# The rarely taken branch of the first MoE at two places: behind the last expert, and behind the fourteenth

## The chip, the cores and the metric

The kernel runs on one core of a Trainium2 chip. The metric is device time in microseconds of one launch. Engines are named as in the profile: PE multiplies matrices (PEld loads its weights, PEq is its sequencer), DVE, ACT and POOL work on vectors, and SP issues most DMA transfers.

## What is computed

Two blocks of two layers each on 256 tokens of width 1024. The change lies in the first block, of which each layer is a token mixer with memory attention, a layer norm, a mixture of experts and a layer norm:

```
def first_block(x, ...):
    for i in range(DEPTH):                       # two layers
        ...                                      # mixer and attention
        x = layer_norm(ALPHA * x + o, ln1_g[i], ln1_b[i])
        f = grouped_moe(x, router_w, router_b, w_gate[i], w_up[i], w_down[i])
        x = layer_norm(ALPHA * x + f, ln2_g[i], ln2_b[i])

def grouped_moe(x, router_w, router_b, w_gate, w_up, w_down):
    ...                                          # combine: two experts of 16 per token
    for e in range(N_EXPERTS):
        h = jax.nn.silu(xt @ w_gate[e]) * (xt @ w_up[e])
        out = out + combine[:, e:e + 1] * (h @ w_down[e])
```

A token goes to two of 16 experts (hidden width 512), so an expert gets some 32 tokens of the 256 on average.

## The kernel before

`moe1` (L923) works off one layer's 16 experts in the loop over `e` at L1025. Tokens of four experts at a time are gathered into at most CAP1 = 64 slots per expert by matmuls with a 0/1 matrix (`gather`). Then come, one iteration apart: `gate_up(e)` (matmuls into tile `gu`, 64 slots against chunks of weights), `hidden(e)` (transposes `tr`), `down(e - 1)` (matmuls `yps`, then tiles `sy` scaled by ACT and DVE) and `scatter(e - 1)`, eight matmuls that add the expert's rows into the four PSUM tiles `ya`. `gate_up` also makes the slot numbers of its expert (`slps`). The tiles `sy` stand in two rooms of the pool `p_c`, tags "lng" and "lnb" (L1013).

The weights come as chunks of 1 MB, six per expert, which SP issues in the order of use (L76) as soon as one of 18 buffers is free (12 called `raw`, 6 called `whl`). Behind the last expert's chunks SP issues the next stage's dense weights and the layer norm's parameters `lngb` (L362).

An expert that more than 64 tokens have chosen is finished by `rest1` (L1065): `most` leaves the largest count in `bigi`, four engines (`BRANCH`: PE, DVE, ACT and SP) read it into a register (L1068), and `tc.If(rv > CAP1)` (L1069) guards a body that runs all 16 experts densely over the tokens left over. With these inputs the body is never taken. Each of the four engines still goes through the `If`: it reads the register, compares, and jumps past the body to a short piece of code that waits until the engine itself (for SP: every transfer that was issued) has finished, adds to the semaphores what the body would have added, and goes on. The scheduler, which otherwise orders instructions by when they can run, moves none across an `If`.

`rest1` is called once per layer, behind the loop (L1041). What follows is `ln_banks` (L505): 24 matmuls on constants that only keep PE running (`warm`, L533), and then for each half t of the tokens: statistics of `ya` on DVE (`bnst`, L521), a chain of small DVE operations that ends in the normalized `pre` (L515), its transposes on PE (`lnT`, L535), their copies on ACT (`xf`, L536) and the first matmuls of the next stage (`begin`). In layer 1 the next stage's first instructions also stand there: on DVE `lp` (L1154), on ACT the DMA issues `gup` (L1132), `strict` and four of `bias` (L1267).

Of the kernel before, what the change touches and what calls it, by code (L numbers as in the profile page):

```python
# [21 lines left out]
T = 256  # L22
ALPHA = 4.0 ** 0.25
E1, F1, CAP1 = 16, 512, 64
# [12 lines left out]
BRANCH = [ET.PE, ET.DVE, ET.Activation, ET.SP]  # L37
# [13 lines left out]
class Stream:  # L51
# [4 lines left out]
    def __init__(self, k, chunks, ahead=1, limit=None, room=None):  # L56
        self.k, self.chunks, self.ahead = k, chunks, ahead
        self.p_raw, self.p_hl, self.small = room or k.p_raw, k.p_hl, room is not None
        self.loaded, self.done, self.pos, self.pool, self.deep = 0, 0, 0, [], 0
        self.raw, self.ready, self.room = [], [], {}  # L60
        self.limit = len(chunks) if limit is None else limit
# [72 lines left out]
class Banks:  # L134
# [5 lines left out]
    def tile(self, shape, dt, name, tag=None):  # L140
        if self.pool is not None and tag not in self.tags:
            return self.pool.tile(shape, dt, name=name, tag=tag)
        self.n += 1
        return self.k.p_ps.tile(shape, dt, name=name, tag=f"b{self.banks[self.n % len(self.banks)]}")


class Begin:
# [81 lines left out]
class Kern:  # L229
# [693 lines left out]
    def moe1(self, layer, stream, x, xt, fill, began, begin):  # L923


        nc, tc = self.nc, self.tc
        pre = self.p_x.tile([128, 2, D], F32, name="pre", tag="x")
        part = lambda e: e == 0 and fill is None
        with ExitStack() as st:
            pool = st.enter_context(tc.tile_pool(name=f"moe{layer}", bufs=1))  # L930
            with ExitStack() as st2:
# [4 lines left out]
                cb, pm, cnt = self.route1(pool, pp, lg)  # L936
# [10 lines left out]
            bigi = self.most(pool, cnt)  # L947
# [3 lines left out]
            bank = lambda t, c: ya[t][c]  # L951
            with ExitStack() as st2:
# [61 lines left out]
                def scatter(e):  # L1014
                    for t in range(2):
                        for c in range(2):
                            if e == 0:
                                self.mm(ya[t][c], self.ident, pre[:, t, half(c, 512)], True, False)
                        for i in range(2):
                            for c in range(2):  # L1020
                                r = half(c, 64)
                                self.mm(ya[t][c], slots[e][0][r, half(t)], ys[e][i][r, :], False, e == E1 - 1 and i == 1)
                    del slots[e], ys[e]

                for e in range(E1 + 1):  # L1025
# [12 lines left out]
                        gb = self.load_ln(2 * layer + 1)  # L1038
                    if e > 0:
                        scatter(e - 1)  # L1040
            self.rest1(layer, bank, x, cb, pm, bigi, part)  # L1041
            xt = self.ln_banks(pre, bank, gb, Banks(self, (0, 1)), begin)
        return pre, xt

# [17 lines left out]
        self.nc.vector.tensor_tensor(w, w, cb, op=OP.mult)  # L1062
        return w

    def rest1(self, layer, bank, x, cb, pm, bigi, part):  # L1065

        nc, tc = self.nc, self.tc
        rv = nc.values_load(bigi[0:1, 0:1], engines=BRANCH, min_val=0, max_val=T)  # L1068
        with tc.If(rv > CAP1):  # L1069
            with ExitStack() as st:  # L1070
                p1 = st.enter_context(tc.tile_pool(name=f"rest{layer}", bufs=1))
                pg, py = Banks(self, (0, 1)), Banks(self, (2, 3))
                room = st.enter_context(tc.tile_pool(name=f"rr{layer}", bufs=2))
                wt = self.left(p1, pm, cb, CAP1, E1)
                xt = self.turned(x, pg, "rg", True)
                for e in range(E1):
                    fs = (1,) if part(e) else (0, 1)
                    w = Stream(self, self.chunks1(layer, e, [j for f in fs for j in (2 * f, 2 * f + 1, 4 + f)]), ahead=0, room=room)
                    self.dense1(w, xt, wt, e, fs, bank, p1, pg, py)
# [572 lines left out]
    def moe2(self, stream, x, xt, began, ln, out):  # L1652
# [5 lines left out]
        with ExitStack() as st:  # L1658
# [191 lines left out]
            def total(t, c, tile):  # L1850
                bank[t][c] = tile()
                self.mm(bank[t][c], self.ident, pre[:, t, half(c, 512)], True, False)
# [21 lines left out]
            for (t, c), tile in zip(halves, tiles):  # L1874
                at(i + 3, total, t, c, tile)
# [349 lines left out]
```

## Time and profile before

| | us |
|---|---|
| three runs | 1952.04, 1956.91, 1957.87 (median 1956.91) |
| profiled execution | 1956.97, of which the span is 1955.2 |
| first MoE, the expert loop up to the last `ya`, layer 0 | about 144 to 386.73 |
| the same, layer 1 | about 530 to 757.36 |
| PE busy over the whole span | 1822.1 (93%) |

The profile is one execution. The span is the time from the first instruction to the last, and the launch has 1.8 us around it. Its times of day ("at 386.73") count from the span's start. [...] DMA is the mean busy share of 16 DMA engines.

### The profile page before, as it was taken

To read this page: it belongs to the slowest core of one execution; us is meant where nothing else is said; L and a number is where in the kernel's file an instruction comes from. 1 tells how busy PE (TensorE), PEld (TensorE's weight loads), DVE (VectorE), ACT (ScalarE), POOL (GpSimd) and SP (SyncE) were. 2 spreads that over 40 slices of the span, in tenths; PEclk is the share of its full clock that TensorE was granted. 3 is DMA by queue.
4 is the path that set the end of the run, shared out by engine and by line. 5 is a ranking of instruction groups with operands and counts; after the bars stand their busy time and mean duration, and the time that the engine had idled before them with its cause. 6 is when DMAs were issued, how large, how long until landed. Compare 5 with 4: busy or idle time off the path is not lost. (4 is left out here: it accounts for less than half of the span.)

```text
span 1955.2 us, 36295 instructions
## 1 busy us (share of the span) xinstructions
PE 1822.1 (93%) x15228; PEld 1424.6 (73%) x15228; DVE 892.0 (46%) x1631; ACT 735.9 (38%) x1205; POOL 297.8 (15%) x129
## 2 busy tenths in 40 slices
PE   9999999899999998998999988899998889999896
PEld 8885555488655555897999867787777778987753
DVE  5661121267411113467101476655556568866412
ACT  5531111054211111652444364344445456655311
POOL 0310000002000000523888323200000000000000
PEclk9999999999999999999999999899999999999898
DMA  9659999855598894744553240489999999899995
GB/s 381 249 193 409 409 419 419 326 198 191 192 414 347 340 419 168 288 169 159 181 187 130 88 177 23 172 323 391 388 416 418 418 419 415 343 391 419 419 415 231
DMA packets 86031, 589.29 MB, mean 301 GB/s; under 512 B 9782, under 2 KB 11510, under 8 KB 16340
## 3 DMA queue, kind: packets, MB, share of 16 engines
q1 hardware_dynamic: 83042, 580.67, 74.6%
q10 hardware_dynamic: 2802, 6.06, 0.9%
q8 instruction: 126, 2.06, 0.4%
q14 instruction: 61, 0.50, 0.1%
HBM read 585.45 MB, written 1.24 MB: 300 GB/s over the span
## 5 line engine op out<-in xcount | busy, mean ns | idle before, releaser
L103 ACT ACTIVATE whl<-raw 128x1024 fp32r<-128x1024 f32 x426 | 433.1, 1054 | 220.4 <-issue 98.4
L105 DVE TENSOR_TENSOR whl<-raw,whl 128x1024 fp32r<-128x1024 f32 x315 | 375.2, 1228 | 128.1 <-ACT whl L103 125.8
L105 POOL TENSOR_TENSOR whl<-raw,whl 128x1024 fp32r<-128x1024 f32 x111 | 274.3, 2489 | 898.5 <-ACT whl L103 845.2
L287 PE MATMUL sgu<-whl,xe 128*128 128x256 f32 x2064 | 261.2, 287 | 27.2 <-DVE sh L1705 21.5
L287 PEld LDWEIGHTS sgu<-whl,xe 128*128 128x128 f32 x2064 | 252.7, 193 | 36.4 <-DVE sh L1705 26.5
L287 PE MATMUL gu<-raw,xe 128*64 128x256 f32 x1408 | 172.4, 382 | 0.0
L287 PEld LDWEIGHTS gu<-raw,xe 128*64 128x64 f32 x1408 | 102.0, 137 | 53.7 <-issue 5.3
L287 PE MATMUL fgu<-xh,whl 128*128 128x256 f32 x640 | 116.7, 283 | 0.0
L287 PE MATMUL zps<-xh,whl 128*128 128x256 f32 x576 | 111.5, 291 | 2.6 <-ACT xh L276 1.8
L990 ACT ACTIVATE h<-gu 128x256 f32<-128x256 f32 x31 | 11.9, 383 | 253.6 <-PE gu L287 253.6
L1948 POOL TENSOR_TENSOR pre<-pre,lngb 128x512 f32<-128x512 f32 x2 | 2.5, 1259 | 672.5 <-ACT pre L1947 672.5
L287 PEld LDWEIGHTS fgu<-xh,whl 128*128 128x128 f32 x640 | 100.3, 192 | 0.4
L991 DVE TENSOR_TENSOR h<-h,gu 128x256 f32<-128x256 f32 x31 | 13.1, 422 | 184.8 <-ACT h L990 184.8
L287 PEld LDWEIGHTS zps<-xh,whl 128*128 128x128 f32 x576 | 92.8, 195 | 3.9 <-ACT xh L276 2.0
L287 PE MATMUL fgu<-xl,whl 128*128 128x256 f32 x320 | 90.4, 283 | 0.0
L287 PE MATMUL yps<-raw,hT 128*64 128x512 f32 x352 | 89.5, 595 | 0.0
L287 PE MATMUL zps<-xl,whl 128*128 128x256 f32 x288 | 82.7, 287 | 0.8 <-DVE xl L277 0.8
L287 PE MATMUL sy<-whl,shh 128*128 128x512 f32 x264 | 82.7, 394 | 0.0
L1688 ACT ACTIVATE sh<-sgu 128x256 f32<-128x256 f32 x43 | 16.5, 383 | 159.1 <-PE sgu L287 159.1
L317 DVE SCALAR_TENSOR_TENSOR sy<-yps,gs,sy 128x512 fp32r<-128x512 f32 x32 | 24.0, 751 | 113.7 <-ACT sy L316 113.7
L287 PE MATMUL gu<-whl,xe 128*64 128x256 f32 x608 | 75.5, 383 | 0.0
L1380 DVE TENSOR_TENSOR fh<-fh,fgu 128x512 f32<-128x512 f32 x10 | 6.9, 689 | 139.7 <-PE fgu L287 139.7
(490 smaller groups left out, 3180.5 us busy)
## 6 DMA issues: line engine op xcount, KB each, us to landing
raw<-in_w_moe_dram SPq DMA_DIRECT2D x399, 1024.0 KB, 11.9
whl<-in_w_moe_dram SPq DMA_DIRECT2D x57, 1024.0 KB, 11.0
raw<-in_w_dense_dram SPq DMA_DIRECT2D x53, 1024.0 KB, 7.0
raw<-in_w_ffn_dram SPq DMA_DIRECT2D x33, 1024.0 KB, 6.0
lngb<-in_lnp_dram ACTq DMA_DIRECT2D x8, 512.0 KB, 4.5
lngb<-in_lnp_dram SPq DMA_DIRECT2D x8, 512.0 KB, 5.0
xraw<-in_xT_dram SPq DMA_DIRECT2D x4, 256.0 KB
raw<-in_w_dense_dram SPq DMA_DIRECT2D x2, 512.0 KB, 4.7
```

What stands on the lines that cost most here:

```text
L103: nc.scalar.activation(hi, r, AF.Copy)
L105: on.tensor_tensor(lo, r, hi, op=OP.subtract)
L287: self.nc.tensor.matmul(out, lhsT, rhs, start=start, stop=stop, skip_group_check=True)
L317: self.nc.vector.scalar_tensor_tensor(yl, ps, gate, yh, op0=OP.mult, op1=OP.subtract)
L990: nc.scalar.activation(h, ps[:, 0, :], AF.Silu)
L991: nc.vector.tensor_tensor(h, h, ps[:, 1, :], op=OP.mult)
L1380: nc.vector.tensor_tensor(h, h, g[1], op=OP.mult)
L1688: nc.scalar.activation(h, ps[:, 0, :], AF.Silu)
L1948: nc.gpsimd.tensor_tensor(v, v, gb[0][:, half(c, 512)], op=OP.mult)
```

## The change

The register is read at the end of the iteration e = 11 (`E1 - 5`), and the `If` stands at the end of the iteration e = 13 (`E1 - 3`), so behind `scatter(12)` and `hidden(13)` and ahead of `gate_up(14)`: twelve chunks, those of the experts 14 and 15, are issued behind it. The body's weights, which stood in two buffers of a pool of their own, take the two rooms "lng" and "lnb" in turn. The body itself is the same. Lines of the changed kernel stand 11 to 14 lower.

```diff
+class InTurn:
+    def __init__(self, pool, tags):
+        self.pool, self.tags, self.n = pool, tags, 0
+
+    def tile(self, shape, dt, name, tag=None):
+        self.n += 1
+        return self.pool.tile(shape, dt, name=name, tag=self.tags[self.n % len(self.tags)])
...
                     if e > 0:
                         scatter(e - 1)
-            self.rest1(layer, bank, x, cb, pm, bigi, part)
+                    if e == E1 - 5:
+                        rv = nc.values_load(bigi[0:1, 0:1], engines=BRANCH, min_val=0, max_val=T)
+                    if e == E1 - 3:
+                        self.rest1(layer, bank, x, cb, pm, rv, part)
             xt = self.ln_banks(pre, bank, gb, Banks(self, (0, 1)), begin)
...
-    def rest1(self, layer, bank, x, cb, pm, bigi, part):
+    def rest1(self, layer, bank, x, cb, pm, rv, part):
         nc, tc = self.nc, self.tc
-        rv = nc.values_load(bigi[0:1, 0:1], engines=BRANCH, min_val=0, max_val=T)
         with tc.If(rv > CAP1):
...
-                room = st.enter_context(tc.tile_pool(name=f"rr{layer}", bufs=2))
+                room = InTurn(self.p_c, ("lng", "lnb"))
```

Three places show what moves. The first is SP in layer 0, from the last two of the MoE's chunks on. Before, the branch stands behind all chunks of the MoE, one dense chunk and the two transfers of `lngb` (`_49` in a wait only numbers the program's semaphores):

```order
L76 DMA raw<-in_w_moe_dram 128x2048 [waits DMAHW4_49,PE_49]
L76 DMA raw<-in_w_moe_dram 128x2048 [waits DMAHW5_49,PE_49]
L76 DMA raw<-in_w_dense_dram 128x2048 [waits DMAHW6_49,PE_49]
L362 DMA lngb<-in_lnp_dram 128x1024 [waits DMAHW7_49,PE_49]
L362 DMA lngb<-in_lnp_dram 128x1024 [waits DMAHW0_49]
L1068 TENSOR_LOAD bigi [waits DVE_49,PE_49,Activation_49]
L1069 COMPARE_AND_BRANCH
```

Now the last chunk of expert 13 stands ahead of the branch:

```order
L76 DMA raw<-in_w_moe_dram 128x2048 [waits DMAHW6_49,PE_49]
L76 DMA raw<-in_w_moe_dram 128x2048 [waits DMAHW7_49,PE_49]
L76 DMA raw<-in_w_moe_dram 128x2048 [waits DMAHW0_49,PE_49]
L76 DMA raw<-in_w_moe_dram 128x2048 [waits DMAHW1_49,PE_49]
L1082 COMPARE_AND_BRANCH
```

and what the engine finds behind the body are the chunks of the experts 14 and 15, of which these are the first seven:

```order
L76 DMA whl<-in_w_moe_dram 128x2048 [waits DMAHW2_49,PE_49]
L76 DMA whl<-in_w_moe_dram 128x2048 [waits DMAHW3_49,PE_49]
L76 DMA whl<-in_w_moe_dram 128x2048 [waits DMAHW4_49,PE_49]
L76 DMA whl<-in_w_moe_dram 128x2048 [waits DMAHW5_49,PE_49]
L76 DMA whl<-in_w_moe_dram 128x2048 [waits DMAHW6_49,PE_49]
L76 DMA whl<-in_w_moe_dram 128x2048 [waits DMAHW7_49,PE_49]
L76 DMA raw<-in_w_moe_dram 128x2048 [waits DMAHW0_49,PE_49]
```

So twelve chunks have moved from the front of the branch to its back. The second place is PE in layer 0 where the branch stands now, between the last four `ya` of `scatter(12)` and, behind the body, the slot numbers and the first `gu` of expert 14:

```order
L298 MATMUL ya_1593<-sy,sT 128x512 [waits DVE_49]
L298 MATMUL ya_1594<-sy,sT 128x512
L298 MATMUL ya_1595<-sy,sT 128x512
L298 MATMUL ya_1596<-sy,sT 128x512
L1053 TENSOR_LOAD bigi [waits DVE_49,PE_49,Activation_49]
L1082 COMPARE_AND_BRANCH
```

and behind the body (the second row of the branch's end is where the four engines add up their counts):

```order
L1082 UNCONDITIONAL_BRANCH
L1082 UNCONDITIONAL_BRANCH [waits PE_49]
L855 MATMUL slps<-consts,pm 128x128 [waits PE_49,Activation_49]
L855 MATMUL slps<-consts,pm 128x128
L855 MATMUL slps<-consts,cb 128x128 x2
L298 MATMUL gu<-raw,xe 64x256 [waits DMAHW0_49,PE_49]
```

Before, those rows of `ya` and `slps` followed each other with nothing between them. The third place is PE at the end of the loop in layer 0. Before, the last `ya` are followed by the branch, and all 24 `warm` stand behind the body:

```order
L287 MATMUL ya_1593<-sy,sT 128x512 [waits DVE_49]
L287 MATMUL ya_1594<-sy,sT 128x512
L287 MATMUL ya_1595<-sy,sT 128x512
L287 MATMUL ya_1596<-sy,sT 128x512
L1068 TENSOR_LOAD bigi [waits DVE_49,PE_49,Activation_49]
L1069 COMPARE_AND_BRANCH
```

and behind the body:

```order
L1069 UNCONDITIONAL_BRANCH
L1069 UNCONDITIONAL_BRANCH [waits PE_49]
L287 LDWEIGHTS bfconst
L287 MATMUL warm<-bfconst 128x256 [waits Activation_49]
L287 LDWEIGHTS bfconst
```

Now no branch stands there, and nine of the 24 `warm` have moved ahead of the last eight `ya`, two of them between the halves of `yps` and seven behind it:

```order
L298 MATMUL yps<-raw,hT 64x512 [waits DMAHW5_49]
L298 MATMUL yps<-raw,hT 64x512 x3
L298 LDWEIGHTS bfconst
L298 MATMUL warm<-bfconst 128x256
L298 LDWEIGHTS bfconst
L298 MATMUL warm<-bfconst 128x256
```

The other 15 follow the last `ya` at once:

```order
L298 MATMUL ya_1593<-sy,sT 128x512 [waits DVE_49]
L298 MATMUL ya_1594<-sy,sT 128x512
L298 MATMUL ya_1595<-sy,sT 128x512
L298 MATMUL ya_1596<-sy,sT 128x512
L298 LDWEIGHTS bfconst
L298 MATMUL warm<-bfconst 128x256
```

What moved there is the branch, which is gone from between `ya` and `warm`. Layer 1 moves in the same way on both engines.

## Rows read from the trace of the kernel before

**Rows 1.** Waits of PE, both layers' loops: line, waited for, us in total, times, longest

```profile
PE ya L287 <- ACT sy L316: 6.3, 9, 0.8
...
PE ya L287 <- ACT sy L316: 5.5, 8, 0.8
```

**Rows 2.** Waits of SP's sequencer, layer 0's loop to its end

```profile
SPq L76 <- PE gu L287: 145.2, 29, 11.9
...
SPq L1069 <- SPq L1069: 11.6, 1, 11.6
```

**Rows 3.** Windows in both loops: each engine's busy time, PEclk, DMA share, GB/s

```profile
339.70:353.10 13.40, 12.56 (x92) 6.44 (x92) 2.09 (x5) 1.34 (x3) 0.00 (x0) 1.00 1.01 418
...
710.30:723.70 13.40, 12.56 (x92) 6.45 (x92) 2.09 (x5) 1.34 (x3) 0.00 (x0) 1.00 1.01 419
```

**Rows 4.** The branch's instructions, layer 0: duration ns min/median/max, first and last start

```profile
L1069 SPq EVENT_SEMAPHORE  x8: 17/17/17, 360.4 to 360.9; - x8
...
L1069 PEldq COMPARE_BRANCH  x1: 6233/6233/6233, 386.7 to 386.7; - x1
```

**Rows 5.** The same view, layer 1

```profile
L1069 PEldq COMPARE_BRANCH  x1: 3549/3549/3549, 757.2 to 757.2; - x1
```

**Rows 6.** Windows at both ends of the loop, columns as in rows 3

```profile
386.73:389.73 3.00, 0.00 (x1) 0.00 (x0) 2.86 (x11) 0.00 (x0) 0.00 (x0) 0.89 1.02 423
389.73:393.11 3.38, 0.00 (x0) 0.03 (x1) 3.31 (x11) 0.00 (x0) 0.00 (x0) 0.50 0.53 206
393.11:396.96 3.85, 3.85 (x24) 2.87 (x25) 3.64 (x16) 0.00 (x0) 0.00 (x0) 0.64 0.02 4
...
757.36:760.87 3.51, 0.00 (x0) 0.03 (x1) 1.09 (x2) 0.00 (x0) 0.00 (x0) 1.00 0.04 9
760.87:765.15 4.28, 4.28 (x24) 3.20 (x25) 4.07 (x18) 0.00 (x0) 0.00 (x0) 0.60 0.32 88
...
767.90:771.30 3.40, 3.36 (x11) 2.89 (x12) 3.29 (x12) 0.84 (x3) 0.00 (x0) 0.50 0.23 62
```

**Rows 7.** Timeline of PE at layer 0's end: start, length, what, [idle before]

```profile
393.11 4.12 PE L287 MATMUL warm<-bfconst 128*128 128x256 bf16 x24 [6.38 <-PEq L1069]
397.06 0.38 PE L535 MATMUL lnT<-consts,pre 128*128 128x128 f32 x2
```

**Rows 8.** Timeline of DVE at layer 0's end

```profile
386.70 1.30 DVE L521 BATCH_NORM_STATS2 bnst<-ya 128x6 f32<-128x512 f32 x2 [0.75 <-DVEq L1069]
...
391.00 1.67 DVE L515 SCALAR_TENSOR_TENSOR pre<-pre,lnrs,lngb 128x256 f32<-128x256 f32 x4
```

**Rows 9.** Timeline of DVE at layer 1's end

```profile
760.91 0.15 DVE L1154 TENSOR_TENSOR lp<-par 64x2 f32<-64x2 f32 x1 [2.46 <-PEq L1069]
```

**Rows 10.** Timeline of ACT and its DMA issues at layer 1's end

```profile
760.89 0.48 ACTq L1132 DMA_DIRECT2D gup<-in_gup_dram  x1
...
761.96 5.50 ACTq L1267 DMA_DIRECT2D bias<-bscr  x4
767.50 0.38 ACT L536 ACTIVATE xf<-lnT 128x256 f32<-128x256 f32 x1 [11.72 <-DVE lnv L405]
```

**Rows 11.** Timeline of SP's issues, layer 0

```profile
301.29 9.53 SPq L76 DMA_DIRECT2D raw<-in_w_moe_dram  x4
313.47 16.43 SPq L76 DMA_DIRECT2D whl<-in_w_moe_dram  x6
```

**Rows 12.** Timeline of SP's issues, layer 1

```profile
677.37 20.31 SPq L76 DMA_DIRECT2D raw<-in_w_moe_dram  x9
```

**Rows 13.** Transfers by name, 300 to 392, then 690 to 724: median us to landing

```profile
raw<-in_w_moe_dram SPq DMA_DIRECT2D x10, 1024.0 KB, 13.7
...
raw<-in_w_moe_dram SPq DMA_DIRECT2D x10, 1024.0 KB, 19.1
```

**Rows 14.** The same view, 346 to 362

```profile
raw<-in_w_dense_dram SPq DMA_DIRECT2D x3, 1024.0 KB, 5.0
```

**Rows 15.** Timeline of PE where expert 14 begins, layer 0

```profile
351.54 1.52 PE L287 MATMUL ya<-sy,sT 64*128 64x512 f32 x8 [0.79 <-ACT sy L316]
...
353.58 3.67 PE L287 MATMUL gu<-raw,xe 128*64 128x256 f32 x32
```

**Rows 16.** The same, layer 1

```profile
724.19 7.13 PE L287 MATMUL gu<-raw,xe 128*64 128x256 f32 x64
```

## The prediction

> **What bounds the kernel now.** The branch is worth what its place is worth, so I read first who waits in the loop. The waits of PE [rows 1] hold one kind only: in either layer `ya` waits some 0.8 us for ACT's `sy`, 9 and 8 times. PE never waits for a chunk. SP waits for PE instead, 145.2 us in 29 places of layer 0, until a buffer is free [rows 2]. The windows say the same: in 13.40 us between two experts PE is busy 12.56 [rows 3]. The DMA share is 1.01 there too, so transfers are always running, but they run ahead. In layer 0 expert 14's first chunk is issued at 313.47 [rows 11], lands 13.7 us later [rows 13], at 327.2, and is used at 353.58 [rows 15], 26 us on. In layer 1 it is the seventh of nine issues 2.5 us apart from 677.37 [rows 12], so 692.4, lands 19.1 us later [rows 13], at 711.5, and is used at 724.19 [rows 16], 12.7 us on. The loop is bound by PE: a microsecond in which PE stands still there is a microsecond of the kernel.
>
> Then the branch itself. On PE the compare lasts 6233 ns in layer 0 [rows 4] and 3549 ns in layer 1 [rows 5], and PE does nothing in it: windows 386.73 to 393.11 and 757.36 to 760.87 [rows 6]. While the jump ran the DMA share was 1.02 for 3 us and then 0.53 in layer 0, and 0.04 in layer 1 [rows 6]. The longer jump is the one beside a full queue. That is two samples, not a law.
>
> Last, what the jump hides today. In layer 0 DVE works on meanwhile: its chain from the last `ya` at 386.70 ends with the first `pre` from 391.00 [rows 8]. So 4.7 us (to 391.4, the first of four `pre`) of the 6.4 would pass on PE in any case. PE starts `warm` only at 393.11, after an idle of 6.38, and `lnT` behind it at 397.06 [rows 7]. In layer 1 DVE's `lp` waits 2.46 us for PE's jump [rows 9], and ACT's `gup` until 760.89; behind it four `bias` issues hold ACT to 767.46, and `xf` starts at 767.50 [rows 10].
>
> **The change part by part.**
>
> *The jump in the loop.* It now lies between `ya` of expert 12 and `slps` of expert 14, at about 353.07 (351.54 + 1.52) in layer 0 [rows 15] and 723.7 in layer 1. Nothing else can run on PE meanwhile, so all of its time is on the path. No row shows a jump at this place. Below: 3.5 us, the jump with a quiet queue. Above: if the 2.7 us between the two samples came in some 4.8 us of busy queue (3.0 + 0.53 x 3.4), a queue busy throughout gives x = 3.55 + 0.56 x, or 8.1 (an estimate). The new place has a DMA share of 1.01 [rows 3], which is nearest to layer 0's row: I take 6.4, twice. 12.8 us lost.
>
> *The clock behind it.* After an idle of 6.4 us layer 0's next 3.85 us of PE ran at a granted clock of 0.64, after 3.5 us layer 1's next 4.28 us at 0.60 [rows 6]: 3.85 x 0.36 = 1.4 and 4.28 x 0.40 = 1.7 us of full-speed work lost. Before, that fell mostly on `warm`. Now it falls on `gu` of expert 14, real work. I take 1.4 per layer (0, if weight loads rather than columns set `gu`'s pace, to 1.7). 2.8 us lost.
>
> *SP's pass.* SP must see every issued transfer land before it issues the twelve chunks of experts 14 and 15. It comes to the branch at about 310.8 in layer 0 [rows 11] and 690 in layer 1, and waits 14 to 19 us. The transfers in flight run on meanwhile, so the queue itself is quiet only from the last landing to the next: a first chunk takes 5.0 us to land [rows 14] where chunks otherwise land every 2.5, and SP needs up to 1 us more, so the stream loses about 3.5 us. The leads of 26 and 12.7 us hide it; without them it would cost 3.5 in each layer. At the old place SP's drain of 11.6 us [rows 2] held only dense chunks and costs nothing now either. Nothing lost or gained.
>
> *The order of `warm`.* Nine of 24 `warm` now stand ahead of the last `ya`. At full speed one takes some 0.10 us (3.85 x 0.64 / 24 [rows 6]), so 0.9 us, of which 0.8 fills the wait for `sy` that stands there. 0.1 to 0.3 per layer: 0.4 lost. The reading of the register at e = 11, and on ACT and DVE the jump beside PE's, cost nothing: of 13.40 us DVE is busy 2.09 and ACT 1.34 [rows 3], and `sy` of expert 13 is not needed until PE has passed.
>
> *The end of layer 0.* `warm` follows `ya` at once and is done before DVE is. `lnT` can start at 391.00 + 1.67 / 4 = 391.4, instead of 396.96: 5.5 us won. Then PE will have been idle some 3 us, and by layer 1's window behind such an idle the next stretch loses up to 1.7; part of it is waiting for DVE and ACT anyway. I take 1.0: 4.5 won (3.8 to 5.5).
>
> *The end of layer 1.* `gup` waits for the last `ya` alone, at 757.36 instead of 760.89, and ACT's issues end 6.6 us later: `xf` at 764.0 instead of 767.50, 3.5 won. DVE's second half comes only 2.46 earlier [rows 9], and the stretch at half clock behind `xf`, from 767.90 [rows 6], stays. I take 3.0 (2.4 to 3.5).
>
> **Sum.** 12.8 + 2.8 + 0.4 - 4.5 - 3.0 = 8.5 us slower: 1956.97 + 8.5 = 1965.5. The profiled execution lies 0.06 above the median of the three runs, so nothing is shifted. The body's two rooms cost nothing, since the body is never run; the pool that goes is room that nobody asks for.
>
> [...]
>
> **Rivals.**
>
> *Faster: the jump in the loop is free.* Either it is short there, or PE catches up because the loop is paced by chunks, and what PE loses it would have spent waiting. Then only the ends remain: 0.4 - 7.5 = -7.1, 1949.9. For it speaks the DMA share of 1.01 in both loops [rows 3]. Against it: it decides only where the lead of the chunks falls to zero, and the leads are 26 and 12.7 us; and both samples of the jump are over 3.5 us. [...]
>
> *No change: the jump is there, but short.* If each costs the 3.5 us of layer 1's row, and `gu` does not feel the clock, 7.0 + 0.4 - 7.5 = -0.1: 1956.9. For it: one of two samples. Against: that sample's queue was quiet, and the new place's is full.
>
> *Slower still: SP's pass starves PE.* If the queue is really empty for as long as SP waits, the 19 us of layer 1 exceed the lead of 12.7 by 6.3, which the jump's 6.4 just covers; 5 us more would show as waits of `gu` for `raw`: about 1970.5. Against it: the landings of what is in flight cover the wait.
>
> *The branch is not where it says.* Some scheduler could push it back. The order of PE rules it out.
>
> **How the numbers follow.** A measurement here tells some 0.3% (5.9 us) from no change. My forecast, 0.58, spreads over jumps of 5.5 to 8.1 and lies mostly over 5.9, with an eighth of it below; the short jump 0.24, of which a third, with some loss to the clock, would still come near the border but under it; starved PE 0.10; free 0.08. Slower is 0.51 + 0.10 = 0.61 and some of the short jump that is longer than its row, 0.03: 0.64; faster 0.08 less what stays within the border, 0.07; same the rest, 0.29. The low end is 3.5 + 3.5 + 0.4 - 9.0 = -1.6, 1955.4; the high end 16.2 + 3.4 + 0.6 - 6.2 = 14.0, 1971, and a little of the starved case, 1973.
>
> **What would show it.** Right: PE idle for 5.5 to 8 us behind `ya` of expert 12 in each layer, waited for by `slps`, then a window at 0.6 to 0.7 of the clock over `gu`; no wait of PE for `raw`; `lnT` in layer 0 some 4.7 us behind the last `ya` instead of 10.3. Wrong: an idle under 4 us in the loop; `gu` at the same pace at half clock; waits of `gu` for `raw`; or `lnT` as late as before.

## The result, and the profile after

The changed kernel takes 1973.19 us (median of 1970.64 to 1974.51, four runs) against 1954.47 for the kernel before in the same comparison: a ratio of 1.0093, 95% interval 1.0075 to 1.0112. It is slower, as forecast, but by 18.7 us and not by 8.5, and the median stands at the very upper end of the range, 1973.

The profiled execution after took 1972.09 us, span 1970.3, 15.1 more than before. Its first 140 us happened to run 4.9 us faster than in the trace of before: the first weights landed sooner (ACT's second `whl`, which waits for them, starts at 7.84 us and not at 9.21) and the granted clock was back at full speed sooner (at 15.35 us and not at 17.00). The other traces of this study are 0.5 to 7.1 us ahead of that of before there, whatever was changed. Behind the end of layer 1, where the work is the same, the trace after loses another 2.9 us; the other traces lie between 0.4 us less and 4.3 us more than before there, so this is not put down to the change. So the two traces are compared stage by stage, from one fixed event to another, and not by times of day.

The timeline of PE after, where the branch now stands in layer 0 (columns as in [rows 15], which answers to it):

```profile
346.60 1.52 PE L298 MATMUL ya<-sy,sT 64*128 64x512 f32 x8 [0.79 <-ACT sy L327]
354.62 0.66 PE L855 MATMUL slps<-consts,pm 128*128 128x128 f32 x2 [6.50 <-PEq L1082]
355.07 0.63 PE L855 MATMUL slps<-consts,cb 128*128 128x128 f32 x2
355.64 5.86 PE L298 MATMUL gu<-raw,xe 128*64 128x256 f32 x32
361.32 3.62 PE L298 MATMUL gu<-whl,xe 128*64 128x256 f32 x32
```

From the start of `ya` to the end of the first 32 `gu` it takes 14.90 us (361.50 - 346.60) where [rows 15] has 5.71: 9.2 us lost, 6.5 of them idle and 2.7 because `slps` and `gu` run slowly (5.86 us for 32 instead of 3.67). The same place in layer 1, which answers to [rows 16], with the `ya` of before ahead of it:

```profile
722.15 1.52 PE L287 MATMUL ya<-sy,sT 64*128 64x512 f32 x8 [0.79 <-ACT sy L316]
```

and after:

```profile
723.26 1.52 PE L298 MATMUL ya<-sy,sT 64*128 64x512 f32 x8 [0.79 <-ACT sy L327]
736.58 0.58 PE L855 MATMUL slps<-consts,pm 128*128 128x128 f32 x2 [11.81 <-issue]
...
737.52 9.51 PE L298 MATMUL gu<-raw,xe 128*64 128x256 f32 x64
```

Here PE stands still for 11.8 us, and the 64 `gu` take 9.51 instead of 7.13. From the start of `ya` to the end of these `gu` it is 23.8 us, and 9.2 before: 14.6 lost. In neither loop does PE wait for a chunk; these are all its waits in layer 0 and in layer 1:

```profile
PE slps L855 <- PEq L1082: 6.5, 1, 6.5
PE ya L298 <- ACT sy L327: 5.5, 8, 0.8
```

```profile
PE slps L855 <- issue: 11.8, 1, 11.8
PE ya L298 <- ACT sy L327: 4.8, 7, 0.8
```

The rows of the branch after, one per layer, with what PE waited for, say how much of that is the jump:

```profile
L1082 PEldq COMPARE_BRANCH  x1: 6197/6197/6197, 348.1 to 348.1; - x1
```

```profile
L1082 PEldq COMPARE_BRANCH  x1: 6027/6027/6027, 724.6 to 724.6; - x1
...
L1082 PEldq EVENT_SEMAPHORE  x1: 51/51/51, 730.7 to 730.7; - x1
```

The jumps are 6.2 and 6.0 us long, as forecast, layer 1's too, which was 3.5 at the old place [rows 5]. But in layer 1 the branch is over at 730.7, and PE issues one weight load and then nothing until 736.58. The profile names no wait there ("issue"). The windows give PEclk, the granted clock of PE as a share of full speed (columns as in [rows 3]). In both traces it is 1.00 or 0.50 at any time, and a value between them is a mean over its window:

```profile
348.10:354.50 6.40, 0.02 (x2) 0.00 (x0) 0.00 (x0) 0.00 (x0) 0.00 (x0) 0.64 1.01 411
354.50:361.30 6.80, 6.68 (x36) 4.06 (x38) 0.92 (x3) 0.00 (x0) 0.00 (x0) 0.59 0.85 339
...
730.80:736.50 5.70, 0.00 (x0) 0.18 (x1) 0.00 (x0) 0.00 (x0) 0.00 (x0) 0.50 1.01 414
736.50:743.50 7.00, 6.92 (x38) 4.12 (x39) 0.92 (x3) 0.00 (x0) 0.00 (x0) 0.58 1.02 420
```

Behind either standstill some 7 us of work ran at 0.58 to 0.59 of the clock: 6.8 x 0.41 = 2.8 and 7.0 x 0.42 = 2.9 us of full-speed work lost.

At the end of layer 0 the gain is there. This answers to [rows 7]:

```profile
389.96 1.51 PE L298 MATMUL ya<-sy,sT 64*128 64x512 f32 x8
391.41 1.81 PE L298 MATMUL warm<-bfconst 128*128 128x256 bf16 x15
396.11 0.44 PE L546 MATMUL lnT<-consts,pre 128*128 128x128 f32 x2 [2.90 <-DVE pre L526]
...
399.52 6.97 PE L298 MATMUL begin<-raw,xf 128*128 128x256 f32 x28
```

`lnT` starts 4.6 us behind the end of `ya`, not 10.3, and now waits for DVE. Behind the idle of 2.9 the 28 `begin` take 6.97 us; before they took 6.21:

```profile
399.50 6.21 PE L287 MATMUL begin<-raw,xf 128*128 128x256 f32 x28
```

So from the end of `ya` to the end of these it is 15.0 us after and 19.0 before: 4.0 won. At the end of layer 1 ACT's issues answer to [rows 10]:

```profile
773.60 0.47 ACTq L1145 DMA_DIRECT2D gup<-in_gup_dram  x1
...
774.67 5.23 ACTq L1280 DMA_DIRECT2D bias<-bscr  x4
780.01 0.38 ACT L547 ACTIVATE xf<-lnT 128x256 f32<-128x256 f32 x1 [8.02 <-DVE pre L526]
```

`ya` ends at 773.55 there, so `xf` comes 6.5 us behind it, where it was 10.1 (767.50 - 757.36). To the end of the first 28 `begin` 3.9 us are won.

### The profile page after: what moved, and what is told of

It is laid out like the page before. It is cut to its first block, busy times and chain, and to the rows that moved or that the text cites. A ratio compares the mean times of both kernels' runs of the same rounds, so it can differ in the third digit from the quotient of the medians.

```text
span 1970.3 us, 36281 instructions
## 1 busy us (share of the span) xinstructions
PE 1827.0 (93%) x15228; PEld 1425.8 (72%) x15228; DVE 891.7 (45%) x1631; ACT 736.5 (37%) x1205; POOL 297.2 (15%) x129
## 5 line engine op out<-in xcount | busy, mean ns | idle before, releaser
L298 PE MATMUL gu<-raw,xe 128*64 128x256 f32 x1408 | 176.9, 390 | 0.0
```

Of the source, the lines that this page charges most:

```text
L298: self.nc.tensor.matmul(out, lhsT, rhs, start=start, stop=stop, skip_group_check=True)
```

## The experiments

**No branch at all, and the branch moved in one layer only.** The first kernel drops the two calls:

```diff
-                    if e == E1 - 5:
-                        rv = nc.values_load(bigi[0:1, 0:1], engines=BRANCH, min_val=0, max_val=T)
-                    if e == E1 - 3:
-                        self.rest1(layer, bank, x, cb, pm, rv, part)
```

> The changed kernel without the fallback branch of the first MoE in either layer (the part of the computation that treats experts with more than 64 tokens is left out; these inputs have none). My theory: what the branch costs is PE's standing still in the jump, the half clock behind it and, in layer 1, a second standstill right behind it; what the place behind the loop cost was only the part that DVE's and ACT's chain did not cover. Then this lies at the kernel before less the two gains at the ends, 4.0 and 3.5 us, plus about 0.5 for the new order of warm: about 1947.5, some 25.5 below the changed kernel. Rival, that the loss of the changed kernel sits in SP's pass through the branch (weights come late): then PE would wait for raw in the changed kernel, and without a branch the loop would also run faster between the experts before the fourteenth.

It takes 1945.27 us against 1957.61 for before (ratio 0.9943, 0.9926 to 0.9960). Its trace, against that of before, wins 3.8 us at layer 0's end and 3.2 at layer 1's, the new order of `warm` counted in, and keeps its distance within 0.05 us in the rest of both loops. The 5 us that remain lie in the first 140 us of its profile, which scatter; how much of them belongs to the runs stays open. The rival, SP's pass, falls with the changed kernel's own trace: SP is in its pass from 305.9 to 320.6 in layer 0, and the distance of PE to the trace of before stays between 4.93 and 4.95 us (after is ahead) from 157 to 352 (times of the trace before), and between 4.24 and 4.26 us (after is behind) from the end of the slow `gu` behind the jump to the scatter of expert 14; PE waits for no chunk.

For the other two the conditions get `layer == 0 and` or `layer == 1 and`, and the other layer calls `rest1` behind its loop.

> Branch behind the fourteenth expert in layer 0 only, behind the loop in layer 1. Theory: layer 0's share as the two traces show it, 9.2 for jump and clock, 0.5 order, 4.0 won at the end: 5.7 slower than before, about 1960. Rival, that both layers cost the same (half of 18.7): 1964.

> Branch behind the fourteenth expert in layer 1 only. Theory: layer 1's share as the two traces show it, 14.6 for jump, second standstill and clock, 3.5 won at the end: 11.2 slower than before, about 1965.5, with an idle of PE of about 11.8 us before slps. Rival, that the second standstill came from something that layer 0's early branch shifted: then 6.4 idle and about 1960.

Layer 0 alone gives 1960.02 (ratio 1.0014, 1.0004 to 1.0023), layer 1 alone 1968.11 (1.0058, 1.0041 to 1.0076). So layer 1 costs the most, and its second standstill is its own: with layer 0's branch at the old place PE still waits as long, but the `gu` behind it take 8.03 us and not 9.51:

```profile
PE slps L855 <- issue: 11.8, 1, 11.8
```

```profile
735.16 8.03 PE L298 MATMUL gu<-raw,xe 128*64 128x256 f32 x64
```

The shares by median (2.4 and 10.5) are lower than the shares by trace (5.7 and 11.2), and their sum is 12.9, not 18.7; the kernels were compared in different sets of runs, whose medians of before went from 1953.9 to 1957.6. In the traces layer 0's place costs 9.2 us again, and layer 1's 13.3 instead of 14.6: the idle is the same, and the clock came back sooner. An unchanged stage can differ as much: with the branch moved in layer 1 only, the end of layer 0 runs 1.4 us longer than in the trace of before.

**The program moved by 32 instructions.** What could stop PE for 5.7 us without a wait? The theory: more of its own program. The kernel is the changed one with 16 more `warm` at layer 0's end, ahead of all that layer 1 does:

```diff
-        self.warm(WARM)
+        self.ends = getattr(self, "ends", 0) + 1
+        self.warm({1: 40, 2: 24}.get(self.ends, WARM))
```

> The changed kernel with 40 instead of 24 warm matmuls at layer 0's end, so that everything behind stands 32 PE instructions later in the program; the 16 lie in PE's idle of 2.9 us there and cost little (up to 0.5). Theory: layer 1's second standstill of 5.7 us right behind the jump is PE waiting for the next stretch of its own program, because the jump's target lies a few instructions before the end of the stretch that was fetched. Moved by 32 instructions the target lies at the beginning of the next stretch and the second standstill goes: PE idle 6.4 before slps of layer 1 instead of 11.8, time about 1967.5. Rival, that PE waits there for another engine or for data: idle stays 11.8, time about 1973.

1965.08 us, ratio 1.0042 (1.0028 to 1.0057). The timeline of PE at layer 1's branch:

```profile
722.57 1.53 PE L298 MATMUL ya<-sy,sT 64*128 64x512 f32 x8 [0.79 <-ACT sy L327]
730.45 0.66 PE L856 MATMUL slps<-consts,pm 128*128 128x128 f32 x2 [6.35 <-PEq L1083]
```

The idle is 6.35 us, not 11.81. The second standstill is gone, with the same data and the same branch and, but for the 16 `warm` some 340 us earlier, the same work, by a shift of the program. Nothing that PE could wait for from others at this place was changed. The time fell by more than these 5.5 us (8.1 by the medians, which come from different sets of runs; 6.6 by the two profiled spans, 1970.3 and 1963.7), and what the rest is stays open.

The traces show what PE waits for there. Beside those of data, the trace lists transfers of a kind "instruction"; those of the queue q8 have 16 KB each. In the changed kernel there are two from 722 to 740 (packets, MB, share):

```profile
q8 instruction: 2, 0.03, 0.7%
```

The first runs from 728.09 to 729.17, and the compare ends at 730.6, 1.4 us later. The second runs from 734.01 to 735.08, and `slps` starts at 736.58, 1.5 us later. In the run with 40 `warm` the second comes as late, from 733.64 to 734.71, but PE has been at work since 730.45 and does not run out of instructions before it. So the second standstill is the wait for the next stretch of PE's program.

The counterpart moves the program the other way, by 16 fewer `warm` at the very start (`WARM0` 14 instead of 30):

> The changed kernel with 14 instead of 30 warm matmuls at the very start, so that the whole program behind stands 32 PE instructions earlier. By my count of the program layer 0's jump then leads where layer 1's led before, a few instructions ahead of the end of a fetched stretch, and layer 1's leads some 38 instructions ahead of one. Theory (PE waits for the next stretch of its program): layer 0 now stands still twice, about 11.8 us instead of 6.5, and layer 1 runs some 38 instructions before it stands still a second time, for 1 to 2 us; time about 1973 to 1976, with the start some 1 us other. Rival (the second standstill belongs to what layer 1 does there): layer 0 stays at 6.5, layer 1 at 11.8.

1976.79 us, 21.8 above before. PE in layer 0, then layer 1:

```profile
358.83 0.66 PE L855 MATMUL slps<-consts,pm 128*128 128x128 f32 x2 [6.28 <-PEq L1082]
...
364.18 4.42 PE L298 MATMUL gu<-raw,xe 128*64 128x256 f32 x22 [1.95 <-issue]
```

```profile
738.64 0.66 PE L855 MATMUL slps<-consts,pm 128*128 128x128 f32 x2 [6.11 <-PEq L1082]
...
744.29 1.97 PE L298 MATMUL gu<-raw,xe 128*64 128x256 f32 x8 [1.81 <-issue]
```

Layer 0 now stands still twice, and layer 1's second standstill moved some instructions on, among the `gu`, and shrank to 1.8 us. Layer 1 does what was expected. Layer 0's second standstill comes, but after some 13 matmuls and for 2 us, not at once and for 5.5: my count of where layer 0's stretch ends was off by some twenty instructions. As in the changed kernel, both second standstills end shortly after a packet of q8 has ended: the packets end at 362.85 and 742.76, and PE goes on at 364.18 and 744.29.

**The rooms alone.** Branch behind the loop as before, weights in "lng" and "lnb".

> The branch behind the loop as before, only its weights in the two rooms lng and lnb. Theory: the rooms cost and bring nothing, since the body is never run: the time of the kernel before within 0.3%, its standstills of 6.4 and 3.5 us too. Rival, that the pool that went or other addresses move something: over 3 us either way.

1955.10 against 1955.03 (0.9998, 0.9987 to 1.0009), with PE's standstill of 6.41 us ahead of `warm` as in [rows 7]. The rooms do nothing; all of the loss is the place.

**A short body.** Is it the jump or its distance? The loop in `rest1` treats one expert instead of 16:

```diff
-                for e in range(E1):
+                for e in range(1):
```

> The changed kernel with a body that treats only the first expert instead of 16 (the rest of the fallback is left out; these inputs never take it). The branch, its barrier and SP's pass stay; PE jumps over some 90 instructions instead of some 1400. Theory, that the jump waits for instructions that were not fetched yet: over so short a distance they are there, the compare takes well under 1 us, no idle and no half clock follow: about 2 us above the kernel without a branch, 1947.5. Rival, that any jump taken costs a load of some 6 us under a full queue, however far it goes: time 1963 to 1973.

> The kernel before with the same short body (15 of 16 experts of the fallback left out), the branch behind the loop. Theory: the jumps of 6.2 and 3.5 us shrink to under 1; lnT of layer 0 starts when DVE is done, lp of layer 1 waits under 1 us: 7 to 9 us faster than before, about 1949. Rival (a jump costs a load at any distance): no change, 1957.

At the new place the rows of PE's branch in layers 0 and 1 are

```profile
L1082 PEldq COMPARE_BRANCH  x1: 358/358/358, 345.9 to 345.9; - x1
```

```profile
L1082 PEldq COMPARE_BRANCH  x1: 219/219/219, 722.7 to 722.7; - x1
```

So a jump over some 90 instructions costs 0.2 to 0.4 us, and one over some 1400 costs 6. That is the distance, not the branch. But the price does not go on growing with it: the second block of the kernel before has a fallback of its own, whose body has some 10,500 instructions of PE, and beside a quiet queue (DMA share 0.04) the jump over it takes as long as layer 1's over 1400:

```profile
L1908 PEldq COMPARE_BRANCH  x1: 3430/3430/3430, 1938.5 to 1938.5; - x1
```

Nor is the whole loss gone with the short body: the time was 1960.35 (1.0024, 1.0009 to 1.0038), not 1947.5: PE stands still a second time all the same, in layer 0 behind the first 6 `gu` for 3.9 us, in layer 1 behind the first 22 for 1.4, and the clock falls behind the longer one,

```profile
347.13 1.08 PE L298 MATMUL gu<-raw,xe 128*64 128x256 f32 x6
352.11 5.70 PE L298 MATMUL gu<-raw,xe 128*64 128x256 f32 x25 [3.91 <-issue]
```

Both standstills end 1.4 us after a packet of q8 (ends at 350.71 and 726.69, PE goes on at 352.11 and 728.06), and from the branch to there the DMA share was 1.00 and 1.02. So behind a short jump, too, the instructions that follow the target came late. At the old place, in layer 0 of the other kernel, the same short jump is followed by

```profile
382.79 2.78 PE L287 MATMUL warm<-bfconst 128*128 128x256 bf16 x24 [0.58 <-PEq L1069]
386.93 0.41 PE L535 MATMUL lnT<-consts,pre 128*128 128x128 f32 x2 [1.35 <-DVE pre L515]
```

and no second standstill shows; `lnT` waits for DVE, 4.7 us behind `ya`. That kernel takes 1948.10 (0.9965, 0.9954 to 0.9975), as expected.

**The jump announced.** An instruction that the trace calls BRANCH_PREFETCH_HINT is put on an engine ahead of its branch. It leaves the whole fallback in place:

```diff
+                    if e == E1 - 1:
+                        for ins, on in ((self.last, ET.PE), (act, ET.Activation), (dve, ET.DVE)):
+                            with tc.issue_after(ins.ins):
+                                tc.mark_branch_hint_location(f"rest{layer}", "LikelyTaken", engines=[on])
...
-        with tc.If(rv > CAP1):
+        with tc.If(rv > CAP1, label=f"rest{layer}"):
```

(`self.last`, `act` and `dve` are the last `gu` matmul and the two operations on `h` of that expert.)

> The kernel before, whole body, branch behind the loop, with one branch prefetch hint each on PE, ACT and DVE behind the last expert's gate and up work (on PE some 4 us ahead of the branch): it names the jump's target so that the engine can fetch it early. Theory, that the jump's time is the wait for instructions that were not fetched: the compare falls to about 0.5 us on PE in both layers, and the time comes to that of the short body at this place, about 1948 against 1955 to 1957 before, with the whole fallback kept. Rival, that the wait is something else in the jump, or that the hint comes too late under a full queue: 3 to 6 us remain and the time stays within 2 us of before.

1949.67 us against 1953.88 (0.9978, 0.9969 to 0.9987): faster than either kernel. The branch of layer 0 in this kernel:

```profile
L1073 ACTq COMPARE_BRANCH  x1: 73/73/73, 383.5 to 383.5; - x1
...
L1073 PEldq COMPARE_BRANCH  x1: 492/492/492, 385.1 to 385.1; - x1
...
L1073 ACTq EVENT_SEMAPHORE  x1: 17/17/17, 389.0 to 389.0; - x1
...
  PE warm L287: 3.9, 1
```

PE's hint is executed at 370.7, 14 us ahead of the branch (not 4, as reckoned). PE's jump falls from 6.2 to 0.49 us, in layer 1 from 3.5 to 0.35. What is left is ACT, which still needs 5.5 us from its compare to the first instruction behind it in layer 0; `warm` waits 3.9 us for it. In layer 1 ACT needs 0.5. So of layer 0's gain about 2 us stay away.

> The changed kernel with the same hints behind the gate and up work of expert 13. Theory: the compare falls to about 0.5 us, but the stretch behind the target is fetched only once the jump is done, under a full queue, so that PE stands still a second time in both layers (3.9 and 1.4 us with the short body) and runs at half clock behind it: about 1960, as the short body at this place, 13 below the changed kernel and still 3 to 5 above before. Rival, that the hint fetches on far enough: about 1948. Second rival, no effect of the hint: 1973.

1961.60 (1.0033, 1.0022 to 1.0044). The time is the one expected, but by another way: no second standstill of PE shows, and `slps` waits for ACT instead, in both layers:

```profile
PE slps L855 <- ACTq L1086: 3.8, 1, 3.8
```

```profile
PE slps L855 <- ACTq L1086: 3.7, 1, 3.7
```

> As the kernel with hints behind the loop, but ACT's hint stands one expert earlier, some 14 us more ahead of its branch. In the last run PE's jump was short, but in layer 0 warm then waited 3.9 us for ACT, whose own jump still took 5.5 us. Theory, that ACT's hint came too late under a full queue: ACT's jump of layer 0 falls under 1 us too, the wait of warm goes, and the time falls by about 2 to some 1947.5. Rival, that ACT's jump there does not follow its hint (it waits for a stretch that the hint does not name): 5.5 us stay, time as in the last run, 1949.7.

1950.05 (0.9974, 0.9963 to 0.9985), no change, with ACT's hint 24 us ahead instead of 10: ACT's jump of layer 0 is as long as before (381.8 to 387.4), so lateness isn't its cause. The hinted kernels together show when ACT's jump stays long: in all four places with a DMA share of 1.02 to 1.04 during it (layer 0 of the two kernels with the branch behind the loop, both layers of the one with it in the loop) ACT needs 5.2 to 5.6 us, and in the two with a share near 0 it needs 0.5. In the four it resumes 1.3 to 1.4 us behind an instruction packet of 8 KB on q14, so there it waits for code that its hint had not brought. Why the hint did not bring it beside a full queue, while PE's hint helped in all six, stays open.

## Why the prediction was right and wrong

*PE bounds the loop: right.* In both loops PE waits for `sy` and for the branch and what follows it, and for no chunk. SP's pass is covered, as the distance of the traces ahead of the fourteenth expert shows. The first rival (free jump, paced by chunks) and the starved PE are out.

*The jump in the loop: right, 6.2 and 6.0 us for 6.4.* The argument that the full queue's row is the nearest held: every jump of PE over the whole body at the new place measured 5.9 to 6.4 us in the study, those over it beside a quiet queue (layer 1 at the old place) 3.5 to 3.7. The rival of a short jump is out.

*Something stood behind the jump that the sum did not have.* My bounds for the jump, 3.5 to 8.1, took the compare for the whole price, and the sum put what follows the target at nothing. In layer 1 a second standstill of 5.7 us follows it, and PE stood still for 11.8. It is the wait for the next stretch of PE's program: by the two shifts of the program the target lay close ahead of the end of the stretch that the jump had fetched, PE issued one weight load behind it, and the next packet of q8 began 5.9 us behind the first. No row of before shows a second standstill. There the next packet began 3.2 and 3.3 us behind the first, with a DMA share of 0.35 and 0.01 in between, and where the target lay in its stretch no row tells; a target close ahead of an end beside a quiet queue was not run. This is the larger part of the miss. The packets of q8, the short body and the shifts agree on it. I had read the trace of before for the jump alone, and not for the instructions that follow it.

*The clock: mechanism right, size wrong.* 2.7 and 2.8 us per layer for 1.4. I took the size from one window at another place: there the clock was back after 2.8 us of work (0.64 over 3.85 us [rows 6] is 72% at the lower level). In the loop it stayed low for 5.6 and 5.9 us of work (0.59 over 6.8 and 0.58 over 7.0). It is no fixed price either: with the branch moved in layer 1 only, the same place lost 1.4 us to it. Why the clock came back sooner in one run than in another no run here settles.

*The order of warm:* the stages in the traces lose 0.5 per layer, forecast 0.2.

*The ends: right.* 4.0 won for 4.5 in layer 0, 3.9 for 3.0 in layer 1; `lnT` 4.6 us behind `ya` for 4.7.

Sum by the traces: 9.2 + 14.6 + 1.0 - 4.0 - 3.9 = 16.9, against 8.5. The second standstill (11.8 of idle for 6.4, so 5.4) and the clock (2.7) make nearly all of the difference; the 1.8 us from 16.9 to the measured 18.7 lie within its interval (14.7 to 21.9). That the time still lies at the end of the range is luck. The parts that I summed ended at 14.0 us, 1971, which is below that interval; the range went on to 1973 only for a PE starved of chunks, and that did not happen.

## What to carry to other kernels

A guarded body that never runs still has a price here: the jump past it waits for code that has not been fetched (3.5 to 6.4 us on PE), and so can the instructions behind the target (1.4 to 5.7 us). Put such a branch where the engine that bounds the kernel would wait for others anyway, not where it is busy and the transfers run at full rate (DMA share 1.0): of layer 0's 6.4 us at the old place 4.7 were covered by DVE's chain, and in the loop all were paid. Before moving it, announce the jump on the engines that go through it (0.9978 here, with the whole fallback) or make the body short (0.9965; the one here left out work that other inputs need). And count what lies behind a wait as well as the wait.

## What the runs showed of the hardware

- PE's jump over some 1400 instructions: 5.9 to 6.4 us at the new place, beside transfers at full rate (DMA share 1.0), and 3.5 to 3.7 beside quiet ones (0.03 to 0.04); over some 10,500, beside quiet ones (0.04, the kernel before), 3.4; over some 90 instructions 0.2 to 0.45; with a hint 0.35 to 0.49.
- Behind the target a second standstill of 1.4 to 5.7 us: 5.7 in layer 1 of the changed kernel and of the one with the branch moved in layer 1 only, none there with the program 32 instructions later, 1.8 with it 32 earlier, 3.9 and 1.4 with the short body. All were seen beside a DMA share of about 1.
- PE's standstills behind a branch in the loop end 1.3 to 1.5 us behind the end of a 16 KB instruction packet on q8. The next such packet began 5.7 to 6.3 us after the first beside a DMA share of about 1, and 3.2 and 3.3 us after it behind the two jumps of the kernel before (DMA share 0.35 and 0.01 in between).
- A hint that worked on PE in six places of six worked on ACT in two, beside a DMA share near 0 (0.5 us), and not in four beside a share of about 1 (5.2 to 5.6 us); 14 us earlier was no better.
- Behind the standstills in the loop 5.6 and 5.9 us of PE's work ran at the lower level of the clock, 2.7 and 2.8 us lost; with the same idle of 11.8 us in another run 1.4.
